# A squared-ReLU MLP whose second product is computed by one level of Strassen's algorithm

## Chip, cores and metric

The kernel runs on one core of a Trainium2 chip, in one launch. The metric is the device time of that launch in microseconds; the median of the runs counts. A profiled execution gives the rows that are read here.

## What is computed

One decoder layer on x of 1024 tokens by 1024 columns, all in float32: adaLN and RMSNorm, a sparse-attention group beside a gated convolution group, an output projection with a gated residual, and then the MLP, which is the part that changes:

```python
x = x + gate1 * mix
h2 = rms_norm(x, norm2) * (1 + scale2) + shift2
ff = jnp.square(jax.nn.relu(h2 @ w_ff1)) @ w_ff2      # 1024 -> 4096 -> 1024
return x + gate2 * ff
```

## The kernel before

**Layout.** Everything is kept transposed: a tile has 128 columns of the layer on the partitions and 512 tokens in the free dimension, so the 1024 tokens are two halves, hf = 0 and 1. TensorE works on float32r operands. Each float32 matrix is split into a hi part (a cast) and a lo part (the matrix less its hi part), and `mm3` (L463) makes three matmuls of every product: hi by hi, hi by lo of the moving operand, lo of the weights by hi. The cast is mostly ScalarE's (L336, or VectorE's at L338), the subtraction VectorE's (L347).

**Planner.** The program text doesn't issue instructions. `Plan.op` records each with its buffers, and an instruction comes to depend on the earlier ones of the text that touch the same part of a buffer. `Plan.issue` (L274) then schedules the list forward and backward several times with a cost for each kind of instruction, takes the shortest schedule, and emits the instructions in that order; engines and the DMA queue of SP keep it. A `Rot` (L400) hands out its buffers in turn, in the order of the program text, so which buffer an instruction uses is fixed before anything is planned. `issue` is called once at the end of the attention stages and once at the end of the MLP stage; nothing moves from one to the other.

**MLP stage** (L1190 to L1251, PSUM tiles pd, eight banks in rotation). The second half's norm comes first: a statistics matmul with bones, `rsqrt_neg2` (L520), and `norm2_apply` (L1069) for each of the eight column tiles, which multiplies (VectorE), scales and shifts (ScalarE) and splits into h[1]. The first half's h2 is there already, in h[0], and so are 30 of its 32 hidden tiles, computed among the attention stages and kept in DRAM as d_hid (NFF = 30). Then four chunks of the inner layer, each 8 tiles of 128 hidden columns:

- First product: for each j, `load_w` (L1203) loads one weight tile of 128x1024, casts it and subtracts; `ff1` (L1214) makes 24 matmuls into a bank, Relu and Square (ScalarE), and `split_hid` splits the result into hid. For the first half only j = 0 and 1 are computed, the other 30 come from d_hid.
- Second product: for each of the 8 output tiles c, one weight tile, and for each half 24 matmuls and one accumulation into x1 by `stt` (VectorE, L358), which multiplies by gate2 and adds. In the last chunk the result is stored.
- After the first chunk's hidden tiles, `ada_cols` computes the eight columns of gate2, from 16 loads of 256 KB.

The buffers for weights as loaded and for working tiles are apart:

```python
ws_r = Fr.rot(2, 8, 128)
tmp, ff_acc = Rot([*Fr.rot(3, 512).t, Gr(512)]), Gr(512)
...
rsqrt_neg2(y1, tmp(), st)
for k in range(8):
    norm2_apply(k, tmp(), x1[k][1], y1, h[1])
```

The second product, with w the split weight tile and hh the split hidden tile:

```python
for hf in range(2):
    a = banks()
    for k in range(8):
        hh = [hid[i][k][hf] for i in range(2)]
        mm3(a, w, hh, S_[:, k], S_[:], k == 0, k == 7)
    P.stt(x1[c][hf], a, mod[:, 40 + c:41 + c], x1[c][hf], mult, add)
```

Of the kernel before, what the change touches and what calls it, by code (L numbers as in the profile page):

```python
# [10 lines left out]
F = mybir.dt.float32  # L11
R = mybir.dt.float32r
AF = mybir.ActivationFunctionType
# [17 lines left out]
S_ = np.s_  # L31


def f32(ap):
    return ap.bitcast(F)
# [398 lines left out]
H0, H1, WR, RAN = 0, 8192, 16384, 16384 + 11328  # L434
AHEAD = {"silu": 30000}
FA1N, FA2N = 13316, 10752

NFF = 30
# [3 lines left out]
def hymba_layer(ctx: ExitStack, tc: tile.TileContext, xT, cT, w_first, w_cols, w_vg, w_ada, w_ada2, b_ada,  # L442
                norm1, norm2, qn, kn, pe, cw1, cw2, conv_w, rel_bias, onehot, ident_c, pair_c, w_out,
                w_ff1, w_ff2, out, dbg=None):
    nc = tc.nc
    P = Plan(tc)
    P.ahead = AHEAD
    mult, add, subt, amax, amin = ALU.mult, ALU.add, ALU.subtract, ALU.max, ALU.min
    EW = ("DVE",)

    def pool(stack, name, side="left", space=None):
        kw = {"space": space} if space else {"side": side}
        if space != DRAM:
            kw["reuse_waits"] = "tile"
        return stack.enter_context(tc.tile_pool(name=name, bufs=1, **kw))
# [7 lines left out]
    def mm3(ps, w, h, wsl, hsl, start, stop):  # L463
        P.mm(ps, w[0][wsl], h[0][hsl], start, False)
        P.mm(ps, w[0][wsl], h[1][hsl], False, False)
        P.mm(ps, w[1][wsl], h[0][hsl], False, stop)
# [4 lines left out]
    def dtile(name, *shape):  # L471
        t = dram.tile(list(shape), F, name=name)
        P.scratch.add(t.tensor.name)
        return t
# [5 lines left out]
    d_hid = [dtile(f"d_hid{j}", 128, 512) for j in range(32)]  # L480
# [5 lines left out]
    def ctile(name, *shape, dtype=F):  # L486
        return const.tile([128, *shape], dtype, name=name)

    bones = ctile("bones", 128, dtype=R)
    mod, bad = ctile("mod", 48), ctile("bad", 48)  # L490
    n1, n2, a1, a2, c1, ct, sl = (ctile(n, 8) for n in ("n1", "n2", "a1", "a2", "c1", "ct", "sl"))
# [7 lines left out]
    RA = keep.tile([128, RAN], R, name="RA")  # L499
    FA1 = keep.tile([128, FA1N], F, name="FA1")  # L500
# [11 lines left out]
    h = [[Region(RA, H0 + 8192 * hf + 4096 * i, H0 + 8192 * hf + 4096 * i + 4096)(8, 512) for i in range(2)] for hf in range(2)]  # L512
# [7 lines left out]
    def rsqrt_neg2(y, t, ms):  # L520

        P.act(t, ms, AF.Ln, bias=eps[0:t.shape[0]])
        P.act(y, t, AF.Exp, scale=-0.5)
        P.act(t, y, AF.Square)
        P.stt(t, ms, EPS, t, add, mult)
        P.stt(y, t, -3.0, y, add, mult)
        return y
# [34 lines left out]
    def ada_cols(j0, n, stage, acc, bank):  # L562

        for k in range(8):
            wa = stage()[:, 0:128 * n]
            P.dma(wa, w_ada2[k, :, 128 * (j0 - 16):128 * (j0 - 16 + n)])
            if k == 0:
                P.act(acc, wa, AF.Copy, scale=sl[:, k:k + 1])
            elif k % 2 == 0:
                P.stt(acc, wa, sl[:, k:k + 1], acc, mult, add)  # L570
            else:
                P.act(wa, wa, AF.Copy, scale=sl[:, k:k + 1])
                P.tt(acc, acc, wa, add, EW)
        for i in range(n):
            P.mm(bank[:, i:i + 1], acc[:, 128 * i:128 * i + 128], one, True, True)
        P.tt(mod[:, j0:j0 + n], bank[:, 0:n], bad[:, j0:j0 + n], add)
# [42 lines left out]
    for k in range(8):  # L619
# [5 lines left out]
        ws = wfs_r()  # L625
# [32 lines left out]
    banks, cbanks = Rot(sc_t), Rot([po_t, fa_t[0], fa_t[1]])  # L658
# [195 lines left out]
    while c0 < TROW:  # L854
        n = min(512, TROW - c0)
        a = cbanks()
# [24 lines left out]
    Gr = Region(FA2, 0, FA2N - 640)  # L881
# [4 lines left out]
    Wr = Region(RA, WR, RAN)  # L886
    fw0_r, hl_r, kall0, q0_r, vt0 = Wr.rot(3, 2, 512), Wr.rot(8, 512), Wr(KC0 + T), Wr.rot(2, 2, 2, 256), Wr(4, 2, 128)
    Wr = Region(RA, RAN - 4160, RAN)
# [180 lines left out]
    def norm2_apply(k, t, x, y, h2):  # L1069
        P.tt(t, x, y, mult, EW)  # L1070
        P.act(t, t, AF.Identity, bias=mod[:, 24 + k:25 + k], scale=a2[:, k:k + 1])
        P.copy(h2[0][:, k], t, ("DVE", "ACT"))
        P.sub(h2[1][:, k], t, f32(h2[0][:, k]), EW)
# [85 lines left out]
    x1 = [[FA1[:, 1024 * c + 512 * hf:1024 * c + 512 * hf + 512] for hf in range(2)] for c in range(8)]  # L1159
    h2 = [h[0], h[1]]  # L1160
    tmp, sacc = Rot(at0), t1_t[1]
# [26 lines left out]


    with ExitStack() as pf:  # L1190
        ff = pool(pf, "ff", side="right")
        psd = pool(pf, "psD", space=PSUM)
        banks = Rot([psd.tile([128, 512], F, name=f"pd{i}") for i in range(8)])
        Fr, Gr = Region(FA1, 8192, FA1N - 1536), Region(FA1, FA1N - 1024, FA1N)
        ws_r = Fr.rot(2, 8, 128)
        tmp, ff_acc = Rot([*Fr.rot(3, 512).t, Gr(512)]), Gr(512)
        w5 = [Region(RA, c, c + 1024)(8, 128) for c in (*range(RAN - 4160, RAN - 1023, 1024), WR)]
        wh_r, wl_r = Rot([w5[0], w5[2], w5[4]]), Rot([w5[1], w5[3]])
        Wr = Region(RA, WR + 1024, RAN - 4160)
        hids = [Wr(512) for _ in range(12)] + [ff.tile([128, 512], R, name=f"hid{i}") for i in range(20)]  # L1200
        hid = [[[hids[16 * hf + 2 * j + i] for hf in range(2)] for j in range(8)] for i in range(2)]

        def load_w(src):  # L1203
            ws, hi, lo = ws_r(), wh_r(), wl_r()
            P.dma(ws, src)
            P.copy(hi, ws)
            P.sub(lo, ws, f32(hi), EW)
            return hi, lo

        def split_hid(j, hf, t):  # L1210
            P.copy(hid[0][j][hf], t, ("DVE",))
            P.sub(hid[1][j][hf], t, f32(hid[0][j][hf]), EW)

        def ff1(j, hf, w):  # L1214
            a = banks()
            for k in range(8):
                mm3(a, w, h2[hf], S_[:, k], S_[:, k], k == 0, k == 7)
            t = tmp()
            P.act(t, a, AF.Relu)
            P.act(t, t, AF.Square)  # L1220
            split_hid(j, hf, t)

        st, y1 = banks(), ff_acc
        P.mm(st, f32(bones), sacc, True, True)
        rsqrt_neg2(y1, tmp(), st)
        for k in range(8):
            norm2_apply(k, tmp(), x1[k][1], y1, h[1])
        for ch in range(4):
            for j in range(8):
                w = load_w(w_ff1[ch * 8 + j])  # L1230
                if ch * 8 + j >= 32 - NFF:
                    t = tmp()
                    P.dma(t, d_hid[ch * 8 + j])
                    split_hid(j, 0, t)
                else:
                    ff1(j, 0, w)
                ff1(j, 1, w)
            if ch == 0:
                for i in range(2):
                    ada_cols(40 + 4 * i, 4, tmp, ff_acc, banks())  # L1240
            for c in range(8):
                w = load_w(w_ff2[ch, c])
                for hf in range(2):
                    a = banks()
                    for k in range(8):
                        hh = [hid[i][k][hf] for i in range(2)]
                        mm3(a, w, hh, S_[:, k], S_[:], k == 0, k == 7)
                    P.stt(x1[c][hf], a, mod[:, 40 + c:41 + c], x1[c][hf], mult, add)
                    if ch == 3:
                        P.dma(out[c, :, hf * 512:hf * 512 + 512], x1[c][hf])  # L1250
        P.issue()  # L1251


# [79 lines left out]
```

## Time and profile before

| | |
|---|---|
| median of 3 runs | 1353.28 us (1350.94 to 1354.62) |
| profiled execution | 1352.0 us, span 1350.2 us, mean granted clock 0.994 |
| PE busy | 1322.4 us, 98% |
| VectorE (DVE) busy | 776.7 us, 58% |
| ScalarE (ACT) busy | 626.6 us, 46% |
| MLP stage | from about 808 us to the end, 542 us |
| moved by DMA | 175.63 MB, mean 130 GB/s |

PE is TensorE, PEld its weight loads, DVE VectorE, ACT ScalarE, SP the queue that issues the transfers. A busy time is a sum over instructions; a share is of the span. Times in rows are microseconds from the start of the span unless marked ns. A matmul's record is longer than the distance to the next one, since they are pipelined.

### The profile page before, as it was taken

How to read it: one execution, taken by the hardware profiler on the slowest of the kernel's cores; microseconds unless marked ns; L12 is line 12 of the kernel's file. 1: busy time of each engine (PE TensorE's matmuls, PEld its weight loads, DVE VectorE, ACT ScalarE, POOL GpSimd, SP SyncE). 2: the span in 40 equal slices, each digit the busy share in tenths (PEclk: the TensorE clock that was granted, in tenths of full speed). 3: DMA queues.
4: the chain of work that ended last, by engine and by line, in shares of the span. 5: the costliest groups of instructions: out<-in, count | busy, mean ns of one | idle time of the engine just before them, and what ended most of it. 6: DMA issues, size and time to landing. Idle time of an engine off the chain costs nothing.

```text
span 1350.2 us, 18276 instructions
## 1 busy us (share of the span) xinstructions
PE 1322.4 (98%) x6424; PEld 1079.6 (80%) x6424; DVE 776.7 (58%) x1882; ACT 626.6 (46%) x1294; POOL 131.5 (10%) x239
## 2 busy tenths in 40 slices
PE   6999999999999999999999999999999999999998
PEld 2788788878878878888888877888888888888887
DVE  6998778868587696565655447543522342244312
ACT  6776677666565597565665435320221032103200
POOL 0001003222221112121112000000000000000000
PEclk9999999999999989999999999999999999999999
DMA  9488895444251315334225523532322241223231
GB/s 331 156 238 237 278 312 186 146 154 135 89 172 57 112 33 169 108 119 145 94 86 172 159 60 102 166 107 86 116 80 61 66 123 63 63 78 94 76 111 63
DMA packets 91601, 175.63 MB, mean 130 GB/s; under 512 B 10746, under 2 KB 30755, under 8 KB 90997
## 3 DMA queue, kind: packets, MB, share of 16 engines
q1 hardware_dynamic: 87764, 159.65, 37.7%
q0 software_dynamic: 3744, 14.81, 3.5%
q8 instruction: 50, 0.82, 0.2%
q14 instruction: 43, 0.34, 0.1%
HBM read 145.48 MB, written 32.61 MB: 132 GB/s over the span
## 4 chain that ended last, share of the span: by engine, by line
PE 88%; DVE 6%; DMA 3%; issue 1%; ACT 1%; SPq 0%; POOL 0%; DVEq 0%; ACTq 0%; POOLq 0%
PE pd L312 39%; PE fa L312 23%; PE sc L312 15%; PE po L312 6%; PE stb L315 3%; PE sc L315 2%; DVE FA L358 2%; DVE RA L347 1%; DVE FA L347 1%; ACT FA L330 1%; DVE FA L377 1%; DMA FA<-in_w_ada 1%; DMA d_tab<-d_row 0%; SPq L397 0%; DMA d_k<-FA 0%
## 5 line engine op out<-in xcount | busy, mean ns | idle before, releaser
L312 PE MATMUL fa<-RA 128*128 128x512 f32 (+1 forms) x1384 | 448.0, 410 | 1.0 <-DVE RA L338 0.7
L312 PE MATMUL pd<-RA 128*128 128x512 f32 x1392 | 409.0, 390 | 0.6 <-DVE RA L338 0.5
L336 ACT CAST RA<-FA 128x512 fp32r<-128x512 f32 (+5 forms) x237 | 163.8, 707 | 459.0 <-PE pd L312 273.0
L312 PE MATMUL sc<-RA 128*128 128x512 f32 (+7 forms) x1328 | 352.3, 367 | 6.8 <-ACT RA L336 2.6
L347 DVE TENSOR_TENSOR RA<-FA,RA 128x512 fp32r<-128x512 f32 (+5 forms) x327 | 248.9, 777 | 141.0 <-PE pd L312 68.4
L312 PE MATMUL pd<-hid,RA 128*128 128x512 f32 x960 | 309.7, 389 | 0.0
L312 PEld LDWEIGHTS pd<-RA 128*128 128x128 f32 x1392 | 261.0, 188 | 56.1 <-issue 1.4
L312 PEld LDWEIGHTS fa<-RA 128*128 128x128 f32 (+1 forms) x1384 | 249.0, 190 | 43.9 <-DVE RA L338 0.9
L312 PEld LDWEIGHTS sc<-RA 128*128 128x128 f32 x1328 | 234.7, 190 | 50.3 <-DVE RA L347 4.6
L312 PEld LDWEIGHTS pd<-hid,RA 128*128 128x128 f32 x960 | 180.2, 188 | 37.4
L358 DVE SCALAR_TENSOR_TENSOR FA<-pd,mod,FA 128x512 f32<-128x512 f32 x64 | 46.4, 746 | 199.8 <-PE pd L312 199.8
L312 PE MATMUL po<-RA 128*128 128x256 f32 (+2 forms) x564 | 140.2, 302 | 0.0
L330 ACT ACTIVATE FA<-FA,nm 128x64 f32<-128x64 f32 (+6 forms) x192 | 114.9, 601 | 24.4 <-DVE nm L366 23.7
L312 PEld LDWEIGHTS po<-RA 128*128 128x128 f32 (+1 forms) x564 | 102.4, 190 | 13.4 <-issue 0.2
L377 DVE CUSTOM_DVE_ANT_0 FA<-sc,FA 128x64 f32<-128x64 f32 (+5 forms) x192 | 84.6, 455 | 43.9 <-PE sc L312 41.3
L330 ACT ACTIVATE FA<-FA 128x512 f32<-128x512 f32 (+2 forms) x147 | 89.9, 619 | 22.3 <-DVE FA L358 12.4
L370 POOL TENSOR_SCALAR FA<-FA,cf 128x640 f32<-128x640 f32 (+8 forms) x115 | 72.6, 642 | 238.5 <-DVE cf L347 136.2
L315 PE MATMUL stb<-FA,FA 128*128 128x128 f32 (+1 forms) x304 | 76.7, 279 | 3.0 <-DVE RA L347 3.0
L347 DVE TENSOR_TENSOR RA<-stb,RA 128x512 fp32r<-128x512 f32 (+1 forms) x84 | 53.3, 635 | 27.9 <-PE po L312 13.2
L315 PE MATMUL sc<-FA,FA 128*128 128x128 f32 (+1 forms) x288 | 68.0, 276 | 0.0
L347 DVE TENSOR_TENSOR RA<-sc,RA 128x512 fp32r<-128x512 f32 (+2 forms) x84 | 51.1, 608 | 25.5 <-ACT RA L336 14.4
L336 ACT CAST RA<-sc 128x512 fp32r<-128x512 f32 (+2 forms) x84 | 43.6, 519 | 38.3 <-PE sc L315 35.3
(126 smaller groups left out, 909.8 us busy)
## 6 DMA issues: line engine op xcount, KB each, us to landing
FA<-in_w_ff SPq DMA_DIRECT2D x64, 512.0 KB, 3.7
FA<-in_w_ada SPq DMA_DIRECT2D x64, 256.0 KB, 3.2
FA<-in_w_ff SPq DMA_DIRECT2D x60, 256.0 KB, 3.0
FA<-in_w_cols SPq DMA_DIRECT2D x34, 256.0 KB, 3.2
FA<-in_xT SPq DMA_DIRECT2D x32, 256.0 KB, 5.2
FA<-in_w_ada SPq DMA_DIRECT2D x16, 512.0 KB, 6.8
d_q<-FA SPq DMA_DIRECT2D x32, 256.0 KB, 4.2
RA<-d_q POOLq DMA_DIRECT2D x16, 512.0 KB, 5.3
```

The costliest lines, as they stand in the source:

```text
L312: self.op([("PE", c, lambda: self.nc.tensor.matmul(out, a, b, start=start, stop=stop))], [out], [a, b])
L315: self.op([("PE", 110.0, lambda: self.nc.tensor.transpose(out, a, ident))], [out], [a, ident])
L330: self.op([("ACT", c, lambda: self.nc.scalar.activation(out, a, func, **kw))], outs, ins)
L336: alts.append((e, 0.833 * n + (53 if ps else 93), lambda: self.nc.scalar.copy(out, a)))
L347: alts.append((e, 1.04 * n + 68, lambda: self.nc.vector.tensor_tensor(out, a, b, op)))
L358: self.op([("DVE", 1.04 * self._n(out) + 68 + 61 * ptr, lambda: self.nc.vector.scalar_tensor_tensor(out, a, s, b, op0, op1, **kw))], [out] ...
L370: alts.append((e, 0.833 * n + 174 + 83 * ptr, lambda: self.nc.gpsimd.tensor_scalar(out, a, s1, s2, op0, op1)))
L377: self.op([("DVE", 1.04 * self._n(out) + 75, lambda: self.nc.vector.tensor_tensor_reduce(out, a, b, 1.0, init, ALU.add, ALU.max, accum))], ...
```

## The change

The second product, in each chunk, is cut into quadrants: the output columns in two (c and c + 4), the inner tiles in two (k = 0 and 1, four tiles each), the tokens in two. Seven products of quadrants take the place of eight (Strassen's algorithm in its form with few additions). A product is `product` for four c, 12 matmuls each. Sums of hidden quadrants and of weight quadrants are made before the split, in float32; sums of products go straight into x1, and u2 collects the two products that three quadrants share, over all chunks, until the last. The hidden tiles are kept unsplit (raw) and split by `split_b` for each product. Weights are loaded as quads of 128x512 (256 KB) in both products of the MLP, 36 quads per chunk for the seven. The first half's j = 0 and 1 of the first product load their weights for themselves. The buffers change: one rotation st_r of six tiles of 512 serves `rsqrt_neg2`, `norm2_apply`, the gate2 columns and the weights as loaded; w_r has 14 tiles for hi and lo parts; b_r three sets for a split quadrant of hidden tiles. The hidden tiles, u2 and y1 lie in one tile FF that takes the place of FA2.

```diff
-        ws_r = Fr.rot(2, 8, 128)
-        tmp, ff_acc = Rot([*Fr.rot(3, 512).t, Gr(512)]), Gr(512)
...
+        raw, u2, y1 = [Fr.rot(8, 512).t for _ in range(2)], Fr.rot(4, 512).t, Fr(512)
+        Fr = Region(FA1, 8192, 12288)
+        st_r, S = Fr.rot(4, 512), Fr.rot(4, 512).t
+        st_r = Rot(st_r.t + Region(FA1, FA1N - 1024, FA1N).rot(2, 512).t)
+        Wr = Region(RA, WR, RAN)
+        w_r = Wr.rot(14, 512)
+        b_r = Rot([*Region(RA, H0, H0 + 8192).rot(2, 2, 4, 512).t, Wr(2, 4, 512)])
+        def split(t):
+            hi, lo = w_r(), w_r()
+            P.copy(hi, t)
+            P.sub(lo, t, f32(hi), EW)
+            return [x.rearrange("p (k n) -> p k n", k=4) for x in (hi, lo)]
+        def split_b(tiles):
+            b = b_r()
+            for k, t in enumerate(tiles):
+                P.copy(b[:, 0, k], t, ("ACT", "DVE"))
+                P.sub(b[:, 1, k], t, f32(b[:, 0, k]), EW)
+            return b[:, 0], b[:, 1]
+        def product(w, x):
             a = banks()
-            for k in range(8):
-                mm3(a, w, h2[hf], S_[:, k], S_[:, k], k == 0, k == 7)
...
+            for k in range(4):
+                mm3(a, w, x, S_[:, k], S_[:, k], k == 0, k == 3)
+            return a
+        def ff1(j, hfs):
+            a = {hf: banks() for hf in hfs}
+            for kk in range(2):
+                w = split(load(st_r(), w_ff1[j][:, 4 * kk:4 * kk + 4]))
+                for hf in hfs:
+                    for k in range(4):
+                        mm3(a[hf], w, h2[hf], S_[:, k], S_[:, 4 * kk + k], kk + k == 0, kk == 1 and k == 3)
+            for hf in hfs:
+                t = raw[hf][j % 8]
+                P.act(t, a[hf], AF.Relu)
+                P.act(t, t, AF.Square)
+        def to_out(c, hf, bank, sign=mod):
+            g = ng[:, c - 4:c - 3] if sign is ng else mod[:, 40 + c:41 + c]
+            P.stt(x1[c][hf], bank, g, x1[c][hf], mult, add)
-        rsqrt_neg2(y1, tmp(), st)
+        rsqrt_neg2(y1, st_r(), st)
         for k in range(8):
-            norm2_apply(k, tmp(), x1[k][1], y1, h[1])
+            norm2_apply(k, st_r(), x1[k][1], y1, h[1])
...
+                if j >= 32 - NFF:
+                    P.dma(raw[0][j % 8], d_hid[j])
+                    ff1(j, (1,))
                 else:
-                    ff1(j, 0, w)
-                ff1(j, 1, w)
+                    ff1(j, (0,))
+                    ff1(j, (1,))
...
+            b11, b12, b21, b22 = raw[0][0:4], raw[1][0:4], raw[0][4:8], raw[1][4:8]
+            def quad(c, f, k, t=None):
+                return load(st_r() if t is None else t, w_ff2[ch, c + 4 * f][:, 4 * k:4 * k + 4])
+            x = split_b(b11)
+            for c in range(4):
+                a = product(split(quad(c, 0, 0)), x)
+                if ch == 0:
+                    P.copy(u2[c], a, ("DVE",))
+                else:
+                    P.tt(u2[c], a, u2[c], add)
+                to_out(c, 0, a)
+            x = split_b(b21)
+            for c in range(4):
+                to_out(c, 0, product(split(quad(c, 0, 1)), x))
...
+            for k in range(4):
+                P.tt(b11[k], b12[k], b11[k], subt)
+            x = split_b(b11)
+            for c in range(4):
+                P.tt(S[c], quad(c, 1, 0, S[c]), quad(c, 1, 1), add)
+                a = product(split(S[c]), x)
+                to_out(c + 4, 1, a)
+                to_out(c, 1, a)
+            for k in range(4):
+                P.tt(b11[k], b22[k], b11[k], subt)
+            x = split_b(b11)
+            for c in range(4):
+                P.tt(S[c], S[c], quad(c, 0, 0), subt)
+                P.tt(u2[c], product(split(S[c]), x), u2[c], add)
+                if ch == 3:
+                    to_out(c, 1, u2[c])
+                    for hf in range(2):
+                        to_out(c + 4, hf, u2[c])
+            x = split_b(b22)
+            for c in range(4):
+                P.tt(S[c], quad(c, 0, 1), S[c], subt)
+                to_out(c, 1, product(split(S[c]), x))
...
+            for k in range(4):
+                P.tt(b12[k], b22[k], b12[k], subt)
+            x = split_b(b12)
+            for c in range(4):
+                t = quad(c, 0, 0)
+                P.tt(t, t, quad(c, 1, 0), subt)
+                a = product(split(t), x)
                 for hf in range(2):
...
+                    to_out(c + 4, hf, a)
...
+            for k in range(4):
+                P.tt(b21[k], b11[k], b21[k], subt)
+            x = split_b(b21)
+            for c in range(4):
+                to_out(c + 4, 0, product(split(quad(c, 1, 1)), x), ng)
```

P1 to P7 are the seven products in the order of the text.

## Rows read from the trace of the kernel before

**Rows 1.** The page's first part: busy us (share of the span) xinstructions.

```profile
PE 1322.4 (98%) x6424; PEld 1079.6 (80%) x6424; DVE 776.7 (58%) x1882; ACT 626.6 (46%) x1294; POOL 131.5 (10%) x239
```

**Rows 2.** The chain that ended last: start, us, engine, tile, line, count.

```profile
815.58 530.35 PE pd L312 x2346
```

**Rows 3.** Stretches of the MLP stage: busy us (xinstructions), PEclk, DMA share, GB/s.

```profile
1000.00:1100.00 100.00, 100.00 (x443) 82.81 (x442) 34.20 (x49) 13.25 (x15) 0.00 (x0) 1.00 0.28 81
1100.00:1200.00 100.00, 100.00 (x442) 82.79 (x442) 29.42 (x38) 19.72 (x25) 0.00 (x0) 1.00 0.21 65
```

**Rows 4.** Instructions on the PSUM tiles pd: duration ns min/median/max, first and last start.

```profile
L312 PE MATMUL pd<-RA x1392: 387/389/796, 809.1 to 1339.9; 128*128 128x512 f32 x199
L312 PE MATMUL pd<-hid,RA x960: 387/389/397, 865.4 to 1345.5; 128*128 128x512 f32 x192
L312 PE MATMUL pd<-one,FA x16: 164/250/250, 881.5 to 894.7; 128*128 128x1 f32 x16
```

**Rows 5.** VectorE in order of time: start, us, line, operation.

```profile
815.35 0.68 DVE L347 TENSOR_TENSOR FA<-FA 128x512 f32<-128x512 f32 x1
815.96 0.68 DVE L347 TENSOR_TENSOR RA<-FA,RA 128x512 fp32r<-128x512 f32 x1
...
1300.40 0.75 DVE L358 SCALAR_TENSOR_TENSOR FA<-pd,mod,FA 128x512 f32<-128x512 f32 x1 [16.77 <-PE pd L312]
1301.07 1.22 DVE L347 TENSOR_TENSOR RA<-FA,RA 128x1024 fp32r<-128x1024 f32 x1
```

**Rows 6.** Stretches around an idle of PE, columns as in rows 3; its matmul after it.

```profile
484.00:486.00 2.00, 0.00 (x0) 0.00 (x0) 1.97 (x7) 1.95 (x5) 0.00 (x0) 1.00 0.62 219
486.00:487.00 1.00, 0.83 (x5) 0.66 (x6) 1.00 (x5) 1.00 (x2) 0.00 (x0) 0.78 0.00 0
487.00:488.00 1.00, 1.00 (x7) 1.00 (x6) 0.97 (x5) 1.00 (x4) 0.00 (x0) 0.50 0.00 0
...
492.00:493.00 1.00, 1.00 (x5) 0.79 (x4) 1.00 (x5) 0.94 (x2) 0.00 (x0) 0.50 0.00 0
493.00:494.00 1.00, 1.00 (x9) 0.93 (x7) 0.86 (x4) 0.96 (x2) 0.04 (x1) 0.81 0.00 0
...
486.17 0.79 PE L315 MATMUL stb<-FA,FA 128*128 128x128 f32 x4 [2.95 <-DVE RA L347]
```

**Rows 7.** ScalarE in order of time: a cast, a scale and shift, a Relu, a Square.

```profile
757.47 0.62 ACT L336 CAST RA<-FA 128x512 fp32r<-128x512 f32 x1
...
817.53 0.81 ACT L330 ACTIVATE FA<-FA,mod,a 128x512 f32<-128x512 f32 x1
...
842.49 0.59 ACT L330 ACTIVATE FA<-pd 128x512 f32<-128x512 f32 x1
843.11 0.63 ACT L330 ACTIVATE FA<-FA 128x512 f32<-128x512 f32 x1
```

**Rows 8.** A stretch early in the kernel, columns as in rows 3.

```profile
12.00:14.00 2.00, 2.00 (x6) 0.81 (x5) 0.35 (x1) 1.43 (x3) 0.00 (x0) 1.00 1.01 407
```

**Rows 9.** DMA issues: count, KB each, median us from issue to landing.

```profile
FA<-in_w_ff SPq DMA_DIRECT2D x60, 256.0 KB, 3.0
```

**Rows 10.** Start of the MLP stage in order of time; last, a stretch of it.

```profile
797.79 1.03 ACT L336 CAST RA<-FA 128x1024 fp32r<-128x1024 f32 x1
...
805.09 0.33 SPq L397 DMA_DIRECT2D d_hid<-FA  x1
...
808.57 1.10 PE L312 MATMUL pd<-FA,bones 128*128 128x512 f32 x2 [2.76 <-DVE FA L347]
...
809.10 5.96 PE L312 MATMUL pd<-RA 128*128 128x512 f32 x22
...
813.20 1.90 DVE L347 TENSOR_TENSOR FA<-FA 128x512 f32<-128x512 f32 x3
...
809.00:811.00 2.00, 2.00 (x9) 1.42 (x8) 0.00 (x0) 1.26 (x2) 0.00 (x0) 1.00 0.97 365
```

**Rows 11.** VectorE, the last instruction of the kernel.

```profile
1345.96 0.75 DVE L358 SCALAR_TENSOR_TENSOR FA<-pd,mod,FA 128x512 f32<-128x512 f32 x1 [0.16 <-PE pd L312]
```

More of the change, by code (lines that the diff above doesn't have):

```diff
@@ L1190, in hymba_layer @@
     with ExitStack() as pf:
-        ff = pool(pf, "ff", side="right")
+        FF = pool(pf, "ff", side="right").tile([128, FA2N], F, name="FF")
         psd = pool(pf, "psD", space=PSUM)
         banks = Rot([psd.tile([128, 512], F, name=f"pd{i}") for i in range(8)])
-        Fr, Gr = Region(FA1, 8192, FA1N - 1536), Region(FA1, FA1N - 1024, FA1N)
-        ws_r = Fr.rot(2, 8, 128)
-        tmp, ff_acc = Rot([*Fr.rot(3, 512).t, Gr(512)]), Gr(512)
-        w5 = [Region(RA, c, c + 1024)(8, 128) for c in (*range(RAN - 4160, RAN - 1023, 1024), WR)]
@@ L1198, in hymba_layer @@
[L1198 to L1214, printed above, removed]
-            a = banks()
-            for k in range(8):
-                mm3(a, w, h2[hf], S_[:, k], S_[:, k], k == 0, k == 7)
[L1218 to L1223, printed above, removed]
+        Fr = Region(FF, 0, FA2N)
+        raw, u2, y1 = [Fr.rot(8, 512).t for _ in range(2)], Fr.rot(4, 512).t, Fr(512)
@@ new lines, in load @@
+        def load(t, src):
+            P.dma(t.rearrange("p (k n) -> p k n", k=4), src)
+            return t
+        def split_b(tiles):
[5 more added lines that the diff above has]
+        def product(w, x):
+            a = banks()
+            for k in range(4):
+                mm3(a, w, x, S_[:, k], S_[:, k], k == 0, k == 3)
+            return a
@@ L1224, in hymba_layer, with store @@
+        def to_out(c, hf, bank, sign=mod):
+            g = ng[:, c - 4:c - 3] if sign is ng else mod[:, 40 + c:41 + c]
+            P.stt(x1[c][hf], bank, g, x1[c][hf], mult, add)
+        def store(c, hf):
+            P.dma(out[c, :, hf * 512:hf * 512 + 512], x1[c][hf])
+        ng = a1[:, 0:4]
+        st = banks()
         P.mm(st, f32(bones), sacc, True, True)
-        rsqrt_neg2(y1, tmp(), st)
+        rsqrt_neg2(y1, st_r(), st)
         for k in range(8):
-            norm2_apply(k, tmp(), x1[k][1], y1, h[1])
+            norm2_apply(k, st_r(), x1[k][1], y1, h[1])
@@ L1228, in hymba_layer @@
         for ch in range(4):
[L1229 to L1234, printed above, removed]
-                else:
-                    ff1(j, 0, w)
-                ff1(j, 1, w)
+            for j in range(8 * ch, 8 * ch + 8):
+                if j >= 32 - NFF:
+                    P.dma(raw[0][j % 8], d_hid[j])
+                    ff1(j, (1,))
+                else:
+                    ff1(j, (0,))
+                    ff1(j, (1,))
@@ L1238, in hymba_layer @@
             if ch == 0:
                 for i in range(2):
-                    ada_cols(40 + 4 * i, 4, tmp, ff_acc, banks())
-            for c in range(8):
-                w = load_w(w_ff2[ch, c])
-                for hf in range(2):
[L1244 to L1250, printed above, removed]
+                    ada_cols(40 + 4 * i, 4, st_r, y1, banks())
@@ new lines, in hymba_layer @@
+                P.ts(ng, mod[:, 44:48], -1.0, None, mult)
+            b11, b12, b21, b22 = raw[0][0:4], raw[1][0:4], raw[0][4:8], raw[1][4:8]
[9 more added lines that the diff above has]
+                to_out(c, 0, a)
@@ new lines, in hymba_layer @@
+            x = split_b(b21)
+            for c in range(4):
+                to_out(c, 0, product(split(quad(c, 0, 1)), x))
+                if ch == 3:
+                    store(c, 0)
+            for k in range(4):
[6 more added lines that the diff above has]
+                to_out(c, 1, a)
@@ new lines, in hymba_layer @@
+            for k in range(4):
[4 more added lines that the diff above has]
+                P.tt(u2[c], product(split(S[c]), x), u2[c], add)
+                if ch == 3:
+                    to_out(c, 1, u2[c])
[5 more added lines that the diff above has]
+                to_out(c, 1, product(split(S[c]), x))
+                if ch == 3:
+                    store(c, 1)
@@ new lines, in hymba_layer @@
+            for k in range(4):
[5 more added lines that the diff above has]
+                a = product(split(t), x)
+                for hf in range(2):
+                    to_out(c + 4, hf, a)
+                if ch == 3:
+                    store(c + 4, 1)
+            for k in range(4):
+                P.tt(b21[k], b11[k], b21[k], subt)
@@ L1251, in hymba_layer @@
+            x = split_b(b21)
+            for c in range(4):
+                to_out(c + 4, 0, product(split(quad(c, 1, 1)), x), ng)
+                if ch == 3:
+                    store(c + 4, 0)
         P.issue()
```

## The prediction

> **What bounds the kernel now.** I read the page's first part, then the chain that ended last, then the stretches of the stage that changes. TensorE is busy 98% of the span, VectorE 58%, ScalarE 46% [rows 1]. The end of the chain of waits is one block: 530.35 us of matmuls into the PSUM tiles pd, 2346 in a row, from 815.58 to the last matmul [rows 2]. So the MLP stage is bound by TensorE alone: its clock is granted in full, PE is busy 100 of 100 us, and VectorE is busy only 34 and ScalarE 13 to 20 of each 100 us [rows 3]. The stage holds 1392 + 960 = 2352 matmuls of 128x512 [rows 4]: 34 tiles of 24 for the first product, 64 of 24 (1536) for the second. The records last 390 ns each because matmuls overlap; what counts is their spacing. 2330 of the 2346 are full size; the 16 tiny ones (the columns of gate2, 0.25 us each as recorded [rows 4]) cost about 2 us together by an estimate from that, so 530.35 - 2 = 528.3 over 2330 gives **0.227 us** per matmul. I use that.
>
> **The change part by part.** The sum is made on the profiled execution: 1352.0 us, span 1350.2; the median of the runs is 1353.28, 1.3 above it, and I add that at the end.
>
> *Matmuls.* Seven products of 4 x 12 matmuls in each of four chunks are 1344, against 1536: 192 fewer, 192 x 0.227 = **-43.6 us**. They are on the path throughout.
> By the Trainium skill (TensorE: Matmul & The Clock Gate, Back-to-back issue gap) a lone 512-column matmul costs about 216 ns and a sustained stream about 131 ns; the trace shows 227 here, so the rule would make of this term -25.2 at 131, and the measurement decides.
>
> *VectorE.* What it does more of is costed by starts, not by durations: a tensor-tensor of 512 columns starts 0.60 us after another (815.35 to 815.96), the accumulation from PSUM takes 0.67 (1300.40 to 1301.07) [rows 5]. In one chunk of the new second product there are 28 lo-parts of the hidden blocks, 16 sums of hidden blocks, 28 lo-parts of weights, 16 sums of weights, 8 additions to u2: 96 x 0.60 = 57.6; and 32 accumulations into x1, 32 x 0.67 = 21.4. Together 79 us, against 336 x 0.227 = 76.3 of TensorE in the same seven products. The first product adds 16 lo-parts, 9.6 us, against 43.6 of TensorE, and sheds the split of its output. So a chunk gives VectorE 89 us in 120: covered on average (74%), not within each product. By product, against 48 x 0.227 = 10.9 of TensorE: P1 9.9, P2 7.5, P3 15.0, P4 12.0, P5 9.9, P6 15.0, P7 9.9. What covers the excess is running ahead (three buffers for hidden blocks, seven pairs for weights) and lagging behind by up to eight PSUM banks; the first product next to it has 34 us to lend. In the last chunk P4 has 12 accumulations more (+8.0) and no first product behind it. From P3 on VectorE has 70 us against 54 of TensorE; a lead of some 18 us (two block sets and seven weight pairs) is just enough. Lower bound of the cost: 0, if the lead is always there; a gain is excluded since VectorE is not on the path now. Upper: each product runs at the slower engine, (4.1 + 1.1 + 4.1) x 4 + 8.0 = 45.2. The nearest row is the dense stretch from 484 to 486, where VectorE is busy 1.97 of 2 us and PE idles 2.95 waiting for it [rows 6]; I take one such gap for the stage, with its clock loss below: **+6.4**.
>
> *ScalarE.* 44 casts of weights and up to 28 of hidden blocks at 0.62 plus 8 x (0.59 + 0.63) are 54 us of 120 in a chunk [rows 7]: beside TensorE, no cost.
>
> *Transfers.* 36 quads of 256 KB per chunk in place of 8 of 512 KB: 9.4 MB in 76.3 us, 124 GB/s; in P3 and P6 eight in 10.9 us, 192 GB/s. The queues moved 407 GB/s early in the kernel [rows 8], a quad lands in 3.0 us [rows 9], and each issue holds SP 0.33 us [rows 10]. Six staging slots turned round in some 7 us give 0.86 quads per us against 0.74 wanted: covered, but by little. No cost taken; what it costs without cover is in the upper bound above.
>
> *The start of the stage.* This is the price that the edit doesn't mention. Before, the weights have staging buffers of their own (ws_r), so the first weight tile is loaded early: it is cast at 797.79, and its 24 matmuls run from 809.10 while norm2 for the second half is still worked out [rows 10]. After, rsqrt_neg2, the eight norm2_apply and the weight loads all draw on one rotation st_r of six: slot 0 for rsqrt_neg2, then 1, 2, 3, 4, 5, 0, 1, 2, so that the first quad of weights falls on slot 3, the one of norm2_apply(2). Its DMA must wait until that step is through. norm2_apply can't start before 813.20 (the first tensor-tensor after the square root) [rows 10]. From there: tensor-tensor 0.68, scale and shift 0.81 [rows 7], cast 0.42, lo-part 0.69 with hand-overs make 815.9; the load lands 3.0 later, 819.0; the cast 0.62 and the hand-over give 820. Nothing else is ready for TensorE: the hidden columns of the first half need the same weights, and the statistics matmul is done at 809.7. Then one quad feeds 2.7 us of matmuls and norm2 frees a slot each 1.2 to 1.5 us, so from there it keeps up. Before, TensorE had done 24 + (820 - 815.58)/0.227 = 43.5 matmuls by 820: 43.5 x 0.227 = **+9.9**. If norm2_apply(2) comes third on VectorE, it is 1.6 more; if the wait isn't there, 0.
> An idle of 10 us costs clock too. After the 2.95 us gap at 486 the clock stood at 0.50 (1.2 GHz) for six rows of 1 us, and at 0.78 and 0.81 in the two beside [rows 6]: 6 x 0.5 + 0.22 + 0.19 = **+3.4** lost. The gap of 2.76 at 808.57 cost no clock [rows 10], which is the other end: 0.
>
> *End.* The last accumulation and store are as before (1345.96 [rows 11] to 1350.2): 0.
>
> Sum: 1352.0 - 43.6 + 6.4 + 9.9 + 3.4 = 1328.1; on the median 1329.4. I say **1329**.
>
> **Rivals.**
> *A, the prefetch is not lost* (the planner finds an order in which first weights come early): 1328.1 - 13.3 = 1314.8, on the median 1316; without VectorE's gap 1309.7. For it: the planner knows every slot. Against: it only orders, it can't give a load another slot, and the slots are drawn in the order of the program text. It is also where the gap is shorter than I think.
> *B, the clock falls in every chunk.* 28 groups of 12 matmuls per chunk change bank twice as often as 16 of 24, and each waits for a fresh pair of weights. One gap as at 486 in each of four chunks (2.95 + 3.4 = 6.4 each, one of them already in the sum) makes 1328.1 + 3 x 6.4 = 1347.3, on the median 1348.6. Against: with eight banks the clock stayed at 1.00 in the stage before [rows 3].
> The Trainium skill (TensorE: Matmul & The Clock Gate, A second HAM failure mode: psum-queue depth-cycling) tells of a kernel whose small idles between groups, while it went round PSUM banks, made the clock swing; by that rule B happens, and the trace so far shows no such swing in this stage.
> *C, slower: VectorE becomes the bound of the seven products.* Price: the upper bound, 1328.1 - 6.4 + 45.2 = 1366.9, on the median 1368. It decides once VectorE's lead is under about one product (11 us): the three block buffers and the rotating slots then tie P3, P4 and P6 to its pace. For it: 79 us against 76.3. Against: 34 us of room in each first product.
> That the change doesn't do what it says is no rival here: the count of matmuls follows from the loops.
>
> **How the numbers follow.** Forecast with its own spread (start stall 7 to 15, VectorE 0 to 15): 0.57, within 1318 to 1340. A 0.20, B 0.11, C 0.12. A difference of 0.3% (4.1 us) is about what a measurement of this kernel can tell from none, so faster means under 1349.2. The forecast and A are faster, B lies on the line and is halved: 0.57 + 0.20 + 0.05 = 0.82; same 0.06; slower, C, 0.12. The range from 1311 to 1350 leaves out C, the lowest part of A and the upper part of B, 0.12 + 0.03 + 0.04.
>
> **What would show it.** Right: 2160 matmuls of 128x512 into pd, still 0.227 apart; an idle of PE of about 10 us near 810 to 820, released through a DMA of in_w_ff and a cast, with the clock at 0.5 behind it; VectorE 70 to 80% busy in the stage; waits of PE for VectorE of single microseconds. Wrong: no idle at 810 (A), a clock under 1 in the later chunks (B), or PE waiting for lo-parts in every P3, P4 and P6 with VectorE over 95% busy there (C); the sum would fail most where VectorE's lead isn't what the buffers allow.

## The result, and the profile after

The changed kernel takes **1321.8 us** (median of 4 runs, 1320.07 to 1324.59) against 1353.83 (4 runs): ratio 0.977, 95% interval [0.975, 0.979]. It was forecast at 1329, within 1311 to 1350. The profiled execution is 1320.07 us, span 1318.3.

The page's first part of the changed kernel answers to [rows 1]:

```profile
PE 1280.0 (97%) x6232; PEld 1043.9 (79%) x6232; DVE 972.1 (74%) x2238; ACT 723.8 (55%) x1503; POOL 132.5 (10%) x239
```

TensorE has 192 matmuls less, VectorE 195 us more, 74% in place of 58%. The chain that ended last answers to [rows 2], and the instructions on pd to [rows 4]:

```profile
812.51 1.90 DVE FA L347 x3
817.51 1.52 ACT FA L330 x2
819.03 1.56 ACT RA L336 x3
820.63 493.54 PE pd L312 x2176
1314.20 0.75 DVE FA L358
```

```profile
L312 PE MATMUL pd<-RA x2160: 387/389/794, 820.6 to 1313.8; 128*128 128x512 f32 x197
...
L358 DVE SCALAR_TENSOR_TENSOR FA<-pd,mod,FA x112: 734/742/753, 884.7 to 1311.2; 128x512 f32<-128x512 f32 x112
```

The end of the chain is again one block of TensorE, 2160 full matmuls and 16 tiny ones without a break, but it starts at 820.63 and before it the chain runs through norm2 on VectorE and ScalarE. The start of the stage in order of time answers to [rows 10] (SPq is the queue that issues the transfers):

```profile
806.83 2.70 SPq L397 DMA_DIRECT2D FF<-d_hid  x6
806.95 2.02 PE L312 MATMUL pd<-FA,bones 128*128 128x512 f32 x2 [2.33 <-DVE FA L347]
...
809.57 1.96 SPq L397 DMA_DIRECT2D FA<-in_w_ff  x4
...
815.26 0.68 DVE L347 TENSOR_TENSOR RA<-FA,RA 128x512 fp32r<-128x512 f32 x1
...
816.00 1.23 SPq L397 DMA_DIRECT2D FA<-in_w_ff  x2
...
820.63 9.72 PE L312 MATMUL pd<-RA 128*128 128x512 f32 x34 [11.66 <-ACT RA L336]
```

PE idles 11.66 us and is released by a cast on ScalarE, of weights that came late. By the program text every staging slot of st_r passes through norm2 before it takes weights, so the four loads at 809.57 must be those that P3 makes straight into S. Behind them the queue stands 4.4 us, until VectorE's lo-part from 815.26 is through and gives the first slot back; at 816.00 the first weights for TensorE are issued.

Stretches of the stage (columns as in [rows 3]) show the clock there and VectorE's load later:

```profile
808.00:812.00 4.00, 0.97 (x2) 0.00 (x0) 0.91 (x2) 1.95 (x3) 0.00 (x0) 0.50 0.90 320
...
820.00:824.00 4.00, 3.37 (x7) 2.32 (x8) 4.00 (x8) 2.56 (x6) 0.00 (x0) 0.50 0.62 190
824.00:828.00 4.00, 4.00 (x19) 3.28 (x18) 3.31 (x6) 2.54 (x5) 0.00 (x0) 0.99 0.83 245
...
900.00:950.00 50.00, 50.00 (x223) 41.40 (x222) 48.30 (x79) 22.45 (x38) 0.00 (x0) 1.00 0.50 153
...
1250.00:1300.00 50.00, 50.00 (x223) 41.40 (x222) 48.61 (x79) 18.23 (x32) 0.00 (x0) 1.00 0.35 116
```

VectorE reaches 48.6 of 50 us in the thick of the products, and PE is still busy 50 of 50 with as many matmuls as before. From the statistics matmul to the end of the span the stage took 1350.2 - 808.57 = 541.6 us before and 1318.3 - 806.95 = 511.4 after, 30.3 less. The rest of the difference of the two spans, 1.6 us, lies ahead of the stage, where the programs are alike.

### The profile page after: what moved, and what is told of

Read it like the earlier page. It is cut to its first block, busy times and chain, and to the rows that moved or that the text cites. A ratio compares the mean times of both kernels' runs of the same rounds, so it can differ in the third digit from the quotient of the medians.

```text
span 1318.3 us, 19010 instructions
## 1 busy us (share of the span) xinstructions
PE 1280.0 (97%) x6232; PEld 1043.9 (79%) x6232; DVE 972.1 (74%) x2238; ACT 723.8 (55%) x1503; POOL 132.5 (10%) x239
## 4 chain that ended last, share of the span: by engine, by line
PE 87%; DVE 6%; DMA 3%; ACT 2%; issue 1%; SPq 1%; DVEq 0%; ACTq 0%
PE pd L312 38%; PE fa L312 23%; PE sc L312 15%; PE po L312 6%; PE stb L315 3%; PE sc L315 2%; DVE FA L358 2%; DVE RA L347 1%; DVE FA L347 1%; ACT FA L330 1%; DMA d_k<-FA 1%; SPq L397 1%; DVE FA L377 1%; DMA FA<-in_w_ada 1%; DMA d_tab<-d_row 0%
## 5 line engine op out<-in xcount | busy, mean ns | idle before, releaser
L312 PE MATMUL pd<-RA 128*128 128x512 f32 x2160 | 492.9, 390 | 11.7 <-ACT RA L336 11.7
L312 PEld LDWEIGHTS pd<-RA 128*128 128x128 f32 x2160 | 406.1, 188 | 97.8 <-ACT RA L336 13.2
L347 DVE TENSOR_TENSOR RA<-FA,RA 128x512 fp32r<-128x512 f32 (+2 forms) x419 | 274.9, 674 | 125.9 <-ACT RA L336 52.9
L336 ACT CAST RA<-FA 128x512 fp32r<-128x512 f32 (+3 forms) x353 | 204.8, 600 | 239.3 <-PE pd L312 133.9
L330 ACT ACTIVATE FA<-FA,nm 128x64 f32<-128x64 f32 (+6 forms) x192 | 114.9, 601 | 24.6 <-DVE nm L366 23.8
L377 DVE CUSTOM_DVE_ANT_0 FA<-sc,FA 128x64 f32<-128x64 f32 (+5 forms) x192 | 84.4, 454 | 43.6 <-PE sc L312 41.3
L336 ACT CAST RA<-FF 128x512 fp32r<-128x512 f32 x93 | 57.8, 622 | 74.1 <-PE pd L312 71.3
L358 DVE SCALAR_TENSOR_TENSOR FA<-pd,mod,FA 128x512 f32<-128x512 f32 x112 | 80.9, 742 | 7.1 <-PE pd L312 7.1
L330 ACT ACTIVATE FA<-FA 128x512 f32<-128x512 f32 (+2 forms) x111 | 67.5, 615 | 21.4 <-DVE FA L358 12.0
L347 DVE TENSOR_TENSOR RA<-FF,RA 128x512 fp32r<-128x512 f32 x112 | 73.9, 683 | 2.7 <-PE pd L312 1.1
L347 DVE TENSOR_TENSOR FA<-FA 128x512 f32<-128x512 f32 (+2 forms) x109 | 71.2, 665 | 4.5 <-ACT FA L330 3.0
```

The lines of the kernel that those rows point to most:

```text
L312: self.op([("PE", c, lambda: self.nc.tensor.matmul(out, a, b, start=start, stop=stop))], [out], [a, b])
L330: self.op([("ACT", c, lambda: self.nc.scalar.activation(out, a, func, **kw))], outs, ins)
L336: alts.append((e, 0.833 * n + (53 if ps else 93), lambda: self.nc.scalar.copy(out, a)))
L347: alts.append((e, 1.04 * n + 68, lambda: self.nc.vector.tensor_tensor(out, a, b, op)))
L358: self.op([("DVE", 1.04 * self._n(out) + 68 + 61 * ptr, lambda: self.nc.vector.scalar_tensor_tensor(out, a, s, b, op0, op1, **kw))], [out] ...
L377: self.op([("DVE", 1.04 * self._n(out) + 75, lambda: self.nc.vector.tensor_tensor_reduce(out, a, b, 1.0, init, ALU.add, ALU.max, accum))], ...
```

## The experiments

The theory: the matmuls give 43.6 us, the shared rotation at the start takes 13.3 of them back, and VectorE is hidden by its lead. Rivals: the late weights are the transfer queue's doing, the new layout has a price of its own, VectorE still costs something, the lead is idle. All edits but the last start from the changed kernel. They were measured in two sets, and the kernel before in each: 1352.62 in the set of own tiles, text order, eight products and no sums, 1353.09 in the set of the others. The changed kernel was in neither, so a distance to it holds within about 1 us. The part ahead of the statistics matmul, whose program text is the same, ends between 806.8 and 811.0 us in these kernels; the stage from there to the end of the span is therefore given too (us, from the profiled executions):

| kernel | before | changed | own tiles, both sets | text order | eight products | no sums | accumulated twice | shorter lead |
|---|---|---|---|---|---|---|---|---|
| stage | 541.6 | 511.4 | 498.8, 497.9 | 500.0 | 554.2 | 513.8 | 533.8 | 532.8 |

**Norm2 with tiles of its own** (u2 isn't used until P1):

```diff
-        rsqrt_neg2(y1, st_r(), st)
+        tn = Rot(u2)
+        rsqrt_neg2(y1, tn(), st)
         for k in range(8):
-            norm2_apply(k, st_r(), x1[k][1], y1, h[1])
+            norm2_apply(k, tn(), x1[k][1], y1, h[1])
```

> The norm2 stage gets working tiles of its own (u2, free until P1); the six staging slots are left to the weights. Slot theory (the late weights at the start of the stage come from sharing the rotation st_r with norm2): the first matmul of the MLP follows the statistics matmul within 1 us, as in the kernel before, the idle of 11.66 us and the stretch at half clock go, and the time is 10 to 13 us under the changed kernel's 1321.8, so 1309 to 1312. Rival, the transfer queue (six loads of d_hid into FF stand in front of the weights and must wait until FA2 is given up): the weights still come only after those, from 809.6, the first matmul at about 813.5, and the gain is under 7 us, 1315 or more.

Measured: **1308.03 us**, ratio 0.967 [0.964, 0.969]; and in the second set:

> The kernel with norm2's own tiles once more, on the same chip as the one before, to compare them: 1308 within 2 us.

1308.9, ratio 0.967 [0.965, 0.968]. Start of the stage in order of time, first set:

```profile
801.79 1.14 ACT L336 CAST RA<-FA 128x512 fp32r<-128x512 f32 x2 [5.24 <-PE fa L312]
...
802.84 0.59 ACT L330 ACTIVATE FA<-fa 128x512 f32<-128x512 f32 x1
...
806.83 1.73 PE L312 MATMUL pd<-FA,bones 128*128 128x512 f32 x2 [2.35 <-DVE FA L347]
807.08 0.43 SPq L397 DMA_DIRECT2D FA<-in_w_ff  x1
...
807.57 22.64 PE L312 MATMUL pd<-RA 128*128 128x512 f32 x91
```

The first weights are cast at 801.79 already, the first MLP matmul follows at 807.57, in place of 820.63, and PE doesn't stop again: the chain ends with one block from 806.83 (in the second set it stops once more, for 0.40 us). The gain is 13.8 and 12.9 us over the changed kernel, by the stage 12.6 and 13.5, with the 11.66 us of idle gone. The transfer queue's rival isn't settled by this run alone, since its loads stand in another order too: weights go out before most of d_hid. The changed kernel's own rows settle it: all six loads of d_hid are issued by 809.53, and what the queue then waits for until 816.00 is a slot.

The casts at 801.79 stand in front of the attention stages' last Relu, at 802.84. So it isn't the case that nothing moves from one `issue` to the other, as was said of the planner; how the two come to overlap, the record doesn't show.

**The same buffers, another order of the text.**

```diff
+        for j in range(32 - NFF):
+            ff1(j, (0,))
         st = banks()
...
                 else:
-                    ff1(j, (0,))
                     ff1(j, (1,))
```

> Same buffers as the changed kernel, only the order of the text: the first half's two hidden tiles (j = 0 and 1) stand before the norm, so that their four quads draw slots 0 to 3 and norm2 draws 4, 5, 0, 1, 2, 3, 4, 5, 0. Slot theory: it is the order in which slots are drawn, not their number; the first weights come early again and the gain is 9 to 13 us, 1309 to 1313. Rival, too few slots: norm2 now waits for the weights' slots to come free, the second half's matmuls come late instead, and the gain is under 6 us, 1316 or more.

Measured: 1310.41 us, ratio 0.968 [0.966, 0.971], 11.4 under the changed kernel. PE in order of time:

```profile
808.93 1.10 PE L312 MATMUL pd<-FA,bones 128*128 128x512 f32 x2 [2.36 <-DVE FA L347]
809.47 4.46 PE L312 MATMUL pd<-RA 128*128 128x512 f32 x17
815.43 7.78 PE L312 MATMUL pd<-RA 128*128 128x512 f32 x33 [1.51 <-ACT RA L336]
823.45 3.03 PE L312 MATMUL pd<-RA 128*128 128x512 f32 x12 [0.24 <-DVE RA L347]
826.87 31.59 PE L312 MATMUL pd<-RA 128*128 128x512 f32 x138 [0.39 <-DVE RA L347]
```

The order in which slots are drawn is the cause, not their number: no buffer was added, and of 11.66 us idle 2.1 are left in three small gaps.

**Eight plain products in the new layout.**

```diff
...
+            for hf, blocks in enumerate(((b11, b21), (b12, b22))):
+                xs = [split_b(t) for t in blocks]
+                for c in range(8):
+                    a = banks()
+                    for kk in range(2):
+                        w = split(quad(c % 4, c // 4, kk))
+                        for k in range(4):
+                            mm3(a, w, xs[kk], S_[:, k], S_[:, k], kk + k == 0, kk == 1 and k == 3)
+                    to_out(c, hf, a)
...
```

> The changed kernel with its buffers, quads and rotations, but the second product as eight plain products of quadrants (two accumulated in one bank), without sums: 2352 matmuls of 128x512 again in place of 2160. If the gain is the matmuls alone: 192 x 0.227 = 43.6 us more than the changed kernel, 1365.4, some 12 us above the kernel before, by the start stall. Rival, the new layout of loads and buffers gives or takes time of its own: the distance differs from 43.6 by more than 4 us.

Measured: 1364.91 us, ratio 1.008 [1.005, 1.011]: 43.1 above the changed kernel (42.8 by the stage) and 12.3 above the one before, which is what the start of the stage costs by the run with own tiles. So quads, rotations and splitting per product cost nothing outside the start, within about 1 us, and the gain is the 192 matmuls. This kernel has no S, and its queue issues no weights between d_hid and 818.68, 8.1 us after the statistics matmul, which fits the reading of the four loads above.

**No sums.** All additions and subtractions of quadrants are dropped, for example

```diff
-            for k in range(4):
-                P.tt(b11[k], b12[k], b11[k], subt)
...
-                P.tt(S[c], quad(c, 1, 0, S[c]), quad(c, 1, 1), add)
+                quad(c, 1, 0, S[c])
+                quad(c, 1, 1)
```

> Leaves out all sums of hidden quadrants and of weight quadrants (32 tensor-tensor instructions of 128x512 in each chunk, 19 us of VectorE per chunk, 77 us in all); every load, split, matmul and accumulation stays. If TensorE alone sets the pace of the chunks: within 2 us of the changed kernel, 1320 to 1324. Rival, VectorE holds TensorE up somewhere (tail of the last chunk, or P3, P4, P6): 4 us or more faster, 1318 or less.

Measured: 1325.2 us, ratio 0.979 [0.976, 0.982], not faster than the changed kernel. One long stretch of the changed kernel, of the one without sums, and of the one with eight products; last, the first matmul of the one without sums:

```profile
850.00:1300.00 450.00, 450.00 (x1995) 372.93 (x1994) 360.51 (x580) 195.16 (x328) 0.00 (x0) 1.00 0.44 138
```

```profile
850.00:1300.00 450.00, 450.00 (x1995) 372.86 (x1994) 286.31 (x459) 185.61 (x318) 0.00 (x0) 1.00 0.43 137
```

```profile
850.00:1300.00 450.00, 450.00 (x1995) 372.92 (x1994) 199.35 (x318) 151.45 (x261) 0.00 (x0) 1.00 0.37 118
```

```profile
824.57 48.42 PE L312 MATMUL pd<-RA 128*128 128x512 f32 x200 [13.24 <-ACT RA L336]
```

VectorE is 74 us lighter, with eight products 161 us, and TensorE makes the same 1995 matmuls. That it is 3 us above the changed kernel, a little outside what was expected, lies in the start: the idle there is 13.24 us against 11.66, its first 200 matmuls take 48.42 against 47.34, and its stage begins 2.6 later; why its start is longer was not pursued.

**More work for VectorE** (every product is then counted twice in the output).

```diff
-            P.stt(x1[c][hf], bank, g, x1[c][hf], mult, add)
+            for _ in range(2):
+                P.stt(x1[c][hf], bank, g, x1[c][hf], mult, add)
```

> Every accumulation into x1 is made twice (the output counts each product twice): 32 more instructions of 0.67 us in each chunk, 36 more in the last chunk's 44, so VectorE has some 110 us per chunk of 120 of TensorE, and 101 in the seven products of 76. Cover theory (a lead of some 18 to 25 us and the room of the first product carry it): the three first chunks cost a few us at most, the last, with no first product behind it, ends 15 to 25 us late: 1335 to 1350. Rival, no cover, each product at the pace of the slower engine: over 100 us more, 1420 or more. Rival, VectorE never matters: 1320 to 1324.

Measured: 1346.42 us, ratio 0.994 [0.993, 0.996], 24.6 above the changed kernel (22.4 by the stage). Stretches, and the last rows of PE and of VectorE:

```profile
1050.00:1100.00 50.00, 50.00 (x223) 41.39 (x222) 50.00 (x81) 19.88 (x34) 0.00 (x0) 1.00 0.46 148
...
1150.00:1200.00 50.00, 50.00 (x222) 41.39 (x221) 50.00 (x80) 19.99 (x34) 0.00 (x0) 1.00 0.45 143
...
1320.00:1345.00 25.00, 1.91 (x8) 1.21 (x7) 20.83 (x32) 0.00 (x0) 0.00 (x0) 0.63 0.23 85
...
1319.79 2.12 PE L312 MATMUL pd<-RA 128*128 128x512 f32 x8 [0.20 <-DVE RA L347]
...
1337.42 3.41 DVE L358 SCALAR_TENSOR_TENSOR FA<-pd,a,FA 128x512 f32<-128x512 f32 x5
```

In the middle chunks VectorE is busy 50.00 of 50 us and TensorE too: the load is carried with no loss. The bill comes at the end, where no first product follows: TensorE is through at about 1322 (from its first matmul on it took some 4 us more than in the changed kernel), and VectorE goes on accumulating to 1340.8. (The last chunk has 44 accumulations, so it has 44 more, not the 36 of the expectation.) That is where the changed kernel's margin ends; its own last accumulations wait for PE, as before.

**A shorter lead.**

```diff
-        w_r = Wr.rot(14, 512)
-        b_r = Rot([*Region(RA, H0, H0 + 8192).rot(2, 2, 4, 512).t, Wr(2, 4, 512)])
+        w_r = Wr.rot(4, 512)
+        b_r = Rot(Region(RA, H0, H0 + 8192).rot(2, 2, 4, 512).t)
```

> Two sets of split hidden blocks in place of three, and two pairs of split weights in place of seven; no work added or left out. Cover theory (it is the lead that hides P3, P4 and P6 on VectorE): with a lead of about one product or less these three run at VectorE's pace, 15 to 45 us more, 1337 to 1367, with idle of PE released by VectorE in each chunk. Rival, the average load decides (VectorE 74% of a chunk) and the lead is idle luxury: 1320 to 1326.

Measured: 1344.22 us, ratio 0.993 [0.991, 0.994], 22.4 above the changed kernel. The size is as expected, the place only in part. Stretches, and rows of PE in order of time:

```profile
850.00:900.00 50.00, 41.26 (x179) 33.84 (x178) 25.84 (x40) 22.74 (x38) 0.00 (x0) 0.90 0.50 158
...
1050.00:1100.00 50.00, 50.00 (x222) 41.12 (x221) 45.51 (x73) 22.11 (x36) 0.00 (x0) 1.00 0.51 164
...
1150.00:1200.00 50.00, 50.00 (x223) 41.37 (x222) 50.00 (x82) 23.14 (x38) 0.00 (x0) 1.00 0.53 173
...
1250.00:1300.00 50.00, 47.61 (x198) 35.84 (x198) 44.04 (x73) 18.55 (x32) 0.00 (x0) 1.00 0.37 122
...
891.16 18.87 PE L312 MATMUL pd<-RA 128*128 128x512 f32 x76 [6.55 <-ACT RA L336]
...
910.92 354.69 PE L312 MATMUL pd<-RA 128*128 128x512 f32 x1558
...
1272.64 6.01 PE L312 MATMUL pd<-RA 128*128 128x512 f32 x24 [0.67 <-DVE RA L347]
```

The second and third chunk lose nothing: from 910.92 on TensorE makes 1558 matmuls without a stop. In the first, PE waits 6.55 us for a cast at 891.16, behind the gate2 columns, whose 16 loads pass through the same staging slots: 43 full matmuls are missing in that stretch against the changed kernel, about 10 us, with the clock at 0.90. That is a price of late weights, not of VectorE's work. In the last chunk 24 are missing in 50 us and 12 more in the next 20, about 8 us together; there TensorE stops about every 24 matmuls, which is what two weight pairs feed, mostly for VectorE's lo-parts and for 0.67 us at most (its weight loads wait 7.1 us for these and 5.0 us for ScalarE's casts). So idle released by VectorE, expected in each chunk, came in the last alone. The edit cuts both the weight pairs and the block sets; which of the two matters was not tested.

**A head start for TensorE** (from the kernel with norm2's own tiles): the first half's two first hidden tiles stand first in the text, and the planner is told to put the statistics matmul behind ten of their matmuls.

```diff
+        n0 = len(P.ops)
+        for j in range(32 - NFF):
+            ff1(j, (0,))
+        head = [o for o in P.ops[n0:] if o.alts[0][0] == "PE"]
         st = banks()
         P.mm(st, f32(bones), sacc, True, True)
+        P.ops[-1].preds.add(head[9])
```

> The kernel with norm2's own tiles, with ten matmuls of the first half's first hidden tile put ahead of the statistics matmul on TensorE (their weights are cast and split by 803.8 there), to fill the 2.35 us in which PE waits for the last square. If that idle and the stretch at a lower clock behind it (mean 0.68 from 808 to 812) are on the path: 2 to 4 us less, 1304 to 1306. Rival, norm2 of the second half sets the start: the statistics come later by as much and PE waits for h[1] instead, no difference, 1307 to 1309.

Measured: 1311.36 us, ratio 0.968 [0.967, 0.970]: 2.5 slower than with own tiles alone, not faster. PE and one cast in order of time:

```profile
810.44 1.10 PE L312 MATMUL pd<-FA,bones 128*128 128x512 f32 x2 [0.97 <-DVE FA L347]
...
814.12 0.62 ACT L336 CAST RA<-FA 128x512 fp32r<-128x512 f32 x1 [4.83 <-DMA FA<-in_w_ff]
...
814.79 44.94 PE L312 MATMUL pd<-RA 128*128 128x512 f32 x190 [3.25 <-ACT RA L336]
```

The idle ahead of the statistics shrinks from 2.35 to 0.97, but the matmul that is next in the planned order waits 3.25 us for a cast, which has waited for a load; loads go out again from 810.69 on. Neither theory had this: at this point not norm2 but a load sets the pace. Only ten matmuls had run by then, so why the plan wants that load so early is open.

## Why the prediction was right

*Matmuls, -43.6.* Right in size and place: 43.1 by the run with eight products. The spacing held: 493.54 us less 2 for the tiny ones is 491.5 over 2160, 0.2276, with a little half-clock in it (0.227 without the 1.7 us below). The Trainium skill (TensorE: Matmul & The Clock Gate, Back-to-back issue gap) gives 216 ns alone and 131 sustained; no run here agrees with 131: both kernels stay at 0.227.

*Start of the stage, +9.9 and +3.4.* Right, and shown twice: own tiles or another order of the text gave back 12.9 to 13.8 and 11.4 us, 13.3 were forecast. The first matmul was put at 820 and came at 820.63, by the path that was worked out: norm2 from 812.51, the weights' load behind it (put at 815.9, issued at 816.00), the cast. That the times agree so closely is in part luck: norm2 began 0.7 us earlier than assumed, and the path from there took 8.1 us in place of 6.8. The split between the two terms was a little off too: after the restart the clock is at 0.50 until 824, which by an estimate from these rows costs 3.4 x 0.5 = 1.7 us, and the statistics matmul itself took 2.02 us in place of 1.10; the rest is idle.

*VectorE, +6.4.* This is the step that failed, by its size: the prediction took one gap like the one at 484 to 486, and there is none. PE isn't stopped once from 820.63 to the end, taking the sums out gains nothing, and the last accumulations wait for PE:

```profile
1307.85 4.06 DVE L358 SCALAR_TENSOR_TENSOR FA<-pd,mod,FA 128x512 f32<-128x512 f32 x6 [2.71 <-PE pd L312]
```

Its lower bound, 0, was the true one. Without this term the prediction's sum for the stage is 541.6 - 43.6 + 13.3 = 511.3, and 511.4 was measured; of the distance between 1329 and 1321.8 under 1 us is left. The row was a poor neighbour: between the engines lie here seven weight pairs, three block sets and eight banks. That such a lead is the cover, and not the mean load alone, is shown for the last chunk only, where the shorter lead lost about 8 us; in the second and third the shorter lead was enough. That the lead suffices there even at 50 of 50 us is shown by the doubled accumulations. The estimate for the last chunk, that VectorE would be just level with TensorE, fits: the 44 accumulations more, 44 x 0.67 = 29 us, made VectorE end 19 us behind TensorE (1 in the changed kernel) and TensorE some 4 us later, so by this estimate it had 7 or 8 us to spare there.

*Rival A* (no lost prefetch) didn't come, but its 1316, less the gap, 1309.7, is what the kernel with norm2's own tiles measures: 1308. *Rival B*: the clock is at 1.00 in every stretch from 828 on, so B didn't come. The trace doesn't agree with the rule of the Trainium skill on cycling through PSUM banks (TensorE: Matmul & The Clock Gate, A second HAM failure mode: psum-queue depth-cycling) either. *Rival C* falls with VectorE's term. *Transfers and ScalarE* cost nothing, as taken: the eight products with 32 quads per chunk and the seven with 36 differ by their matmuls alone, within about 1 us.

## What to carry to other kernels

Where an engine at 98% bounds a stage, as here, counting its instructions and taking their spacing (not their recorded length) gave the gain of an algorithm that needs fewer, and the work moved to an engine with a lower mean load was hidden by buffers that let it run ahead. Look first at the stage's two ends: there the shorter lead and the doubled accumulations cost time, and in the middle neither did. When a change merges buffers into one rotation, go through the order in which slots are drawn: a load that could be made early is then tied to the last user of its slot, and the order of the text decides who that is. Here that trap cost 13 of 44 us, and four spare tiles gave them back: 1308 us, the fastest kernel of this study.

## Unexpected

The clock after the idle ahead of the statistics matmul was not the same from kernel to kernel. The first row is of the kernel with eight products, the other two are of the two sets of own tiles:

```profile
810.55 1.10 PE L312 MATMUL pd<-FA,bones 128*128 128x512 f32 x2 [2.33 <-DVE FA L347]
```

```profile
808.00:812.00 4.00, 4.00 (x13) 2.90 (x12) 1.83 (x3) 3.40 (x7) 0.00 (x0) 0.68 0.87 290
```

```profile
808.00:812.00 4.00, 2.52 (x9) 1.81 (x10) 1.39 (x3) 1.97 (x4) 0.00 (x0) 1.00 0.49 150
```

In the kernel before, 2.76 us of idle at 808.57 left it at 1.00 [rows 10]; in the changed kernel 2.33 us of idle at 806.95 were followed by 0.50, and the matmul took 2.02 us in place of 1.10; in the kernel with eight products the same 2.33 us left the matmul at 1.10 us. The two sets of runs of the kernel with norm2's own tiles differ in the same way, 0.68 and 1.00 from 808 to 812, with times within 1 us. So a price for an idle of two to three microseconds can be given here only within bounds; what decides between them, the runs don't show.
